# One exponential for both directions of a chunked scan: a predicated copy in PSUM in place of additive bars

## The chip, the cores and the metric

The kernel runs on one core of one Trainium2 chip. The time is the device time of one execution in microseconds (us). One execution of the kernel before was recorded by the hardware profiler; the rows below come from it. Engines are named as the profile names them: PE is TensorE's matmul side and PEld its weight loads, DVE is VectorE, ACT is ScalarE, POOL is GpSimd, SP issues most of the transfers. A number such as L1104 is a line of the kernel before.

## What is computed

The program is one layer of an encoder block: a modulated RMS norm, one input projection, grouped-query attention, a bidirectional Mamba-2 scan, two output projections merged by gates, and an MLP. The change touches the scan alone. Its part of the reference, cut:

```python
def segsum(a):
    cs = jnp.cumsum(a, axis=-1)
    diff = cs[..., :, None] - cs[..., None, :]
    return jnp.where(tril_mask, diff, -jnp.inf)

def ssd_chunked(xdt, a, bm, cm):                   # chunks of 128 positions
    CB = jnp.einsum("bclgn,bcsgn->bgcls", Cc, Bc)
    M = CB[:, :, None] * jnp.exp(segsum(A))
    y_diag = jnp.einsum("bgrcls,bcsgrp->bclgrp", M, X)
    ...                                            # states, carried from chunk to chunk
    return y_diag + y_off

y = ssd_chunked(forward) + flip(ssd_chunked(flipped, backward)) + ssd_D[:, None] * xf
```

Within a chunk, an output position l takes from a position s at or before it with the forward weights and from a position s at or after it with the backward weights. A pair off the diagonal therefore has one of the two weights, and a pair on the diagonal has both: there the difference of the cumulated sums is zero, so each direction's weight is that direction's dt times CB.

## The kernel before

The sequence of 1024 positions is 8 chunks of 128; the 32 scan heads are 4 groups of 8. The stage in question runs two streams that are woven into one order for PE: `scan()`, which goes through 4 x 8 = 32 pairs of group and chunk, and `products()`, which does the last gate columns and the two output projections, 24 matmuls of 128x512 for each half tile (L206 to L208). PE's order is fixed by `weave`, which takes the next piece from the stream that is behind by the planned costs. The orders of the other engines are set by the scheduler of the framework from dependences and priorities. Every engine runs its own list in order.

For one pair, `scan_load` loads the chunk, multiplies B and C to CB (PSUM tile `psm`, L1089) and lets ACT copy it to `cb` (L1091). `scan_w` is called twice, for four heads each. For each direction d it puts a block of 128x512 into a PSUM tile `psd`: first a product of the identity `identr` with `bars[d]` (L1104), which writes 0 where the direction counts and -1e30 where it doesn't; then a product of `st` and `mv` (L1105), which adds the differences of the cumulated sums (and the logarithm of dt). ACT takes the exponential into an SBUF tile `e` (L1107). DVE adds the two `e` tiles to `w` and multiplies `w` by `cb` (both recorded on the helper's line L154). There are two `psd` buffers, so a direction's product waits for the exponential of the same direction in the call before.

The rest of a pair follows one turn of the loop later. `scan_off` starts the output `u` on POOL as x times D (`Dbc`) and adds the two carried parts: a product `pso` on PE (L1122), a scaling `yo` on DVE, an addition on POOL. `scan_state` carries the forward state (`prevf`), `bwd_stream` prepares the backward states of the next group (`prevb`). `scan_y` multiplies `w` by x (`psy`, L1148), DVE adds it to `u`, POOL multiplies by `sz`, and one turn later PE transposes `u` (`psm`, L1158) in `scan_out`. The tiles `psm`, `pso`, `pst` and `psy` share four PSUM buffers (`psx`). While the second output projection begins, `load_g` fetches the finished scan results and splits them: `gh` on ACT (L1014), `gl` on DVE (L1015).

Of the kernel before, what the change touches and what calls it, by code (L numbers as in the profile page):

```python
# [9 lines left out]
F32 = mybir.dt.float32  # L10
F32R = mybir.dt.float32r
BF16 = mybir.dt.bfloat16
AF = mybir.ActivationFunctionType
ALU = mybir.AluOpType
# [4 lines left out]
P = 128  # L19
S = 1024  # L20
D = 1024
# [4 lines left out]
HD = 64  # L26
# [30 lines left out]
M2 = {mybir.EngineType.PE}  # L57
LEAD3 = 400
BIG = 1.5 * 2.0 ** 15
BAR = 1e30  # L60


def weave(tc, *streams, lead=0):
# [27 lines left out]
def block(ctx: ExitStack, tc: tile.TileContext, ia, out, upto=99, dbg=None):  # L91
    nc = tc.nc
    V, A, G, T = nc.vector, nc.scalar, nc.gpsimd, nc.tensor
# [39 lines left out]
    ident, GT, LT, LE, GE = (masks[:, i, :] for i in range(5))  # L133
# [12 lines left out]
    dt = sp.tile([P, NT, 64], F32, name="dt")  # L146
# [3 lines left out]
    def bc(ap, shape):  # L150
        return ap.to_broadcast(shape)

    def tt(e, o, a, b, op):
        e.tensor_tensor(out=o, in0=a, in1=b, op=op)  # L154
# [102 lines left out]
    with tc.tile_pool(name="p0", bufs=1) as p0, tc.tile_pool(name="ps0", bufs=1, space=PSUM) as ps0:  # L257
# [4 lines left out]
        ps = ps0.tile([P, 512], F32, name="psv", tag="psv", bufs=2)  # L262
# [97 lines left out]
        ps = ps0.tile([P, 512], F32, name="psv", tag="psv", bufs=2)  # L360
# [56 lines left out]
    with tc.tile_pool(name="p1", bufs=1, reuse_waits="tile") as p1, \  # L417
# [16 lines left out]
        identr = p1.tile([P, P], F32R, name="identr")  # L434
# [582 lines left out]
    with tc.tile_pool(name="p4", bufs=1, reuse_waits="tile") as p4, \  # L1017
# [8 lines left out]
        for q in range(2):  # L1026
            dma(pick[20 + 4 * q:24 + 4 * q], ia["pick"][0:4])

        identr = p4.tile([P, P], F32R, name="identr")
        V.tensor_copy(identr, ident)  # L1030
        bars = [p4.tile([P, 4, P], F32R, name=f"bar{d}") for d in range(2)]
        for d, m in enumerate((LE, GE)):
            V.tensor_scalar(out=bars[d], in0=bc(m.unsqueeze(1), [P, 4, P]), scalar1=-1.0, scalar2=BAR, op0=ALU.add, op1=ALU.mult)
        for i in range(2):
            for d in range(2):

# [3 lines left out]
        Dbc = p4.tile([P, NSH], F32, name="Dbc")  # L1040
# [25 lines left out]
        def scan_load(g, c):  # L1066

            hs = slice(8 * g, 8 * g + 8)
            e = dict(g=g, c=c, hs=hs)
            xb = p4.tile([P, 640], F32, name="xb", tag="xb", bufs=2)  # L1070
            dma(xb, xb_d[g][:, c])
            e["xt"], bt = xb[:, 0:512].rearrange("p (h d) -> p h d", h=8), xb[:, 512:640]
            bcT = p4.tile([P, 2, P], F32, name="bcT", tag="bcT", bufs=2)
            dma(bcT, bc_d[g][:, :, c * P:(c + 1) * P])
            bT, e["cT"] = bcT[:, 0], bcT[:, 1]
            e["st"], e["mv"] = cst[cnt[0] % 2], cmv[cnt[0] % 2]
            cnt[0] += 1
            r0 = c * 8 + 2 * g
            for d in range(2):
                dma(e["st"][d][0:28].bitcast(F32), cn_d[d][:, r0:r0 + 2])  # L1080
                dma(e["mv"][d][4:20:5].bitcast(F32), cr_d[d].rearrange("q (h r) l -> q h r l", h=4)[:, :, r0:r0 + 2])
            e["prevb"] = None
            if c < 7:
                e["prevb"] = p4.tile([P, 8, HD], F32, name="pbl", tag="pbl", bufs=2)
                dma(e["prevb"].rearrange("p h d -> p (h d)"), pb_d[g][c])
            e["sz"] = p4.tile([P, 512], F32, name="sz", tag="sz", bufs=2)
            dma(e["sz"], z_d[g][:, c])
            ps = ps4.tile([P, 512], F32, name="psm", tag="psx", bufs=PSX)
            T.matmul(ps[:, :P], bT, e["cT"], start=True, stop=True)  # L1089
            e["cb"] = p4.tile([P, P], F32, name="cb", tag="cb", bufs=2)  # L1090
            A.copy(e["cb"], ps[:, :P])  # L1091
            if c < 7:
                e["xd"] = p4.tile([P, 8, HD], F32, name="xdf", tag="xd", bufs=3)
                tt(G, e["xd"], e["xt"], bc(dec["sf"][:, c, hs].unsqueeze(2), [P, 8, HD]), ALU.mult)
            e["bt"] = bt
            e["w"] = []
            return e

        def scan_w(e, hh):

            ex = []
            for d in range(2):
                pd = ps4.tile([P, 512], F32, name="psd", tag="psd", bufs=2)
                T.matmul(pd, identr, bars[d].rearrange("p h l -> p (h l)"), start=True, stop=False)  # L1104
                T.matmul(pd.rearrange("p (h l) -> p h l", h=4), e["st"][d][:, hh], e["mv"][d][:, :, hh], start=False, stop=True)  # L1105
                ex.append(p4.tile([P, 4, P], F32, name="e", tag="e", bufs=3))
                A.activation(ex[d].rearrange("p h l -> p (h l)"), pd, AF.Exp)  # L1107
            wh = p4.tile([P, 4, P], F32, name="w", tag="w", bufs=4)
            e["w"].append(wh)
            tt(V, wh, ex[0], ex[1], ALU.add)  # L1110
            tt(V, wh, wh, bc(e["cb"].unsqueeze(1), [P, 4, P]), ALU.mult)

        def scan_off(e, prev, ed):

            c, hs = e["c"], e["hs"]
            if "u" not in e:
                e["u"] = p4.tile([P, 8, HD], F32, name="u", tag="u", bufs=2)
                tt(G, e["u"], e["xt"], bc(Dbc[:, hs].unsqueeze(2), [P, 8, HD]), ALU.mult)
            if prev is None:
                return  # L1120
            po = ps4.tile([P, 8, HD], F32, name="pso", tag="psx", bufs=PSX)
            T.matmul(po.rearrange("p h d -> p (h d)"), e["cT"], prev.rearrange("p h d -> p (h d)"), start=True, stop=True)  # L1122
            t = p4.tile([P, 8, HD], F32, name="yo", tag="yo", bufs=2)
            tt(V, t, po, bc(ed[:, c, hs].unsqueeze(2), [P, 8, HD]), ALU.mult)
            tt(G, e["u"], e["u"], t, ALU.add)
# [51 lines left out]
        def scan():  # L1177
# [5 lines left out]
            for g in range(NG):  # L1183
                bw = bwd_stream(g + 1) if g + 1 < NG else iter(())
                for c in range(NT + (2 if g == NG - 1 else 0)):
                    e = None
                    if c < NT:
                        e = scan_load(g, c)
                        yield 0.43
                        scan_w(e, 0)  # L1190
                        yield 0.43
                    if p:
                        scan_off(p, f, dec["ef"])
                        yield 0.85
                    if o:
                        scan_out(o)
                        pipe["done"] += 1
                        yield 0.85
                    if p:
                        scan_off(p, p["prevb"], dec["eb"])  # L1200
                        yield 0.85
                        f = scan_state(p, f)
                        yield 0.85
                    if e:
                        scan_w(e, 1)
                        yield 0.43
                    if p:
                        scan_y(p)
                        yield YC
                    if next(bw, None):  # L1210
                        yield 0.85
                    o, p = p, e
# [40 lines left out]
    with tc.tile_pool(name="p5", bufs=1, reuse_waits="tile") as p5, \  # L1253
# [41 lines left out]
        for n, (i, second) in enumerate(jobs):  # L1295
# [12 lines left out]
            for half in range(2):  # L1308
                ps = part[i][half] if i in part else ps5.tile([P, 512], F32, name="psg", tag="psg", bufs=6)
# [39 lines left out]
    with tc.tile_pool(name="p6", bufs=1, reuse_waits="tile") as p6:  # L1349
# [9 lines left out]
        def turned(hf, k):  # L1359
            ps = ps7.tile([P, 512], F32, name="pst", tag="ps1", bufs=4)  # L1360
            for j in range(4):
                T.transpose(ps[:, j * P:(j + 1) * P], x1[hf * 4 + j][:, k * P:(k + 1) * P], ident)
            return ps
# [4 lines left out]
        for t in range(NT):  # L1368
# [3 lines left out]
            for n in range(2):  # L1372
# [3 lines left out]
                ps = ps7.tile([P, 512], F32, name="pso", tag="ps2", bufs=4)  # L1376
# [12 lines left out]
            if t == 4:  # L1389
                for k in range(KT):  # L1390
                    ps = turned(0, k)
# [404 lines left out]
```

## Time and profile before

| | us |
|---|---|
| median of 3 runs | 2523.82 |
| the 3 runs | 2523.82, 2516.72, 2524.56 |
| the profiled execution | 2523.71 |
| its span, first to last instruction | 2521.9 |
| PE busy in the span | 2418.8 (96%) |
| DVE busy | 1724.4 (68%) |
| ACT busy | 1125.7 (45%) |
| POOL busy | 867.8 (34%) |

The profiled execution lies at the median, and 1.8 us of it lie outside the span. PE is busy nearly everywhere; the scan stage is the stretch from about 1229 to 1641 us. A matmul's busy time includes the part in which the next one already runs, so what a matmul takes of PE's time is read from the distance between starts.

### The profile page before, as it was taken

How to read it: one execution, taken by the hardware profiler on the slowest of the kernel's cores; microseconds unless marked ns; L12 is line 12 of the kernel's file. 1: busy time of each engine (PE TensorE's matmuls, PEld its weight loads, DVE VectorE, ACT ScalarE, POOL GpSimd, SP SyncE). 2: the span in 40 equal slices, each digit the busy share in tenths (PEclk: the TensorE clock that was granted, in tenths of full speed). 3: DMA queues.
4: the chain of work that ended last, by engine and by line, in shares of the span. 5: the costliest groups of instructions: out<-in, count | busy, mean ns of one | idle time of the engine just before them, and what ended most of it. 6: DMA issues, size and time to landing. Idle time of an engine off the chain costs nothing. (4 is left out here: it accounts for less than half of the span.)

```text
span 2521.9 us, 32355 instructions
## 1 busy us (share of the span) xinstructions
PE 2418.8 (96%) x11403; PEld 1937.3 (77%) x11403; DVE 1724.4 (68%) x2199; ACT 1125.7 (45%) x1944; POOL 867.8 (34%) x672
## 2 busy tenths in 40 slices
PE   5899999999999999999899999998998999999999
PEld 5898777888867777777577767776776888888887
DVE  5756345777766666666577787546569888667794
ACT  5455522555466666666333444343233222264430
POOL 3210107666501111110356565514017866113200
PEclk9899999999999999999999999999999999999999
DMA  7654661333622222111766665466414544564422
GB/s 261 187 163 130 211 202 61 99 101 117 193 96 80 63 75 69 51 57 38 250 198 204 187 207 170 130 225 196 145 65 163 201 153 164 191 198 141 152 84 88
DMA packets 282162, 363.38 MB, mean 144 GB/s; under 512 B 33673, under 2 KB 166513, under 8 KB 282001
## 3 DMA queue, kind: packets, MB, share of 16 engines
q1 hardware_dynamic: 209841, 285.22, 36.2%
q10 hardware_dynamic: 72160, 76.11, 9.1%
q8 instruction: 90, 1.47, 0.3%
q14 instruction: 71, 0.58, 0.1%
HBM read 248.18 MB, written 113.06 MB: 143 GB/s over the span
## 5 line engine op out<-in xcount | busy, mean ns | idle before, releaser
L892 DVE TENSOR_REDUCE nm<-pss 128x1 f32<-128x1024 f32 x128 | 156.6, 1224 | 133.9 <-PE pss L890 132.4
L380 PE MATMUL psq<-twl,hh 128*128 128x400 f32 (+1 forms) x512 | 194.2, 381 | 5.5 <-DVE twl L154 4.8
L379 PE MATMUL psq<-twh,hh 128*128 128x400 f32 (+1 forms) x512 | 193.5, 383 | 3.4 <-ACT qkvr L512 1.2
L381 PE MATMUL psq<-twh,hl 128*128 128x400 f32 (+1 forms) x512 | 192.7, 378 | 0.2 <-DVE hl L154 0.2
L894 ACT ACTIVATE pf<-pss,nm 128x1024 f32<-128x1024 f32 x128 | 142.8, 1115 | 102.0 <-PE pst L905 99.3
L154 DVE TENSOR_TENSOR pl<-pst,ph 128x512 fp32r<-128x512 f32 x256 | 167.8, 683 | 27.6 <-ACT ph L168 27.6
L905 PEld LDWEIGHTS pst<-masks,pf 128*128 128x128 f32 x1024 | 118.4, 140 | 70.0 <-issue 29.6
L168 ACT CAST ph<-pst 128x512 fp32r<-128x512 f32 x256 | 146.4, 585 | 54.2 <-PE pst L905 41.0
L905 PE MATMUL pst<-masks,pf 128*128 128x128 f32 x1024 | 157.0, 276 | 11.7 <-DVE pl L154 9.7
L1673 PE MATMUL p<-o,o 128*128 128x512 f32 x400 | 153.6, 390 | 2.2 <-DVE ac L154 1.4
L1674 PE MATMUL p<-o,o 128*128 128x512 f32 x400 | 155.3, 389 | 0.2 <-DVE o L154 0.2
L154 POOL TENSOR_TENSOR av<-av,rz 64x512 f32<-64x512 f32 x32 | 41.5, 1298 | 326.6 <-DMA rz<-rz 168.3
L1675 PE MATMUL p<-o,o 128*128 128x512 f32 x400 | 153.7, 389 | 0.0
L714 DVE SCALAR_TENSOR_TENSOR tap<-pad,cwT,tap 128x1024 f32<-128x1024 f32 x96 | 123.4, 1285 | 5.1 <-ACT tap L712 3.7
L168 ACT CAST wop<-ws 128x512 fp32r<-128x512 f32 x116 | 71.8, 620 | 112.7 <-PE pp L1333 77.3
L380 PEld LDWEIGHTS psq<-twl,hh 128*128 128x128 f32 x512 | 99.0, 193 | 18.1 <-DVE twl L154 5.8
L154 POOL TENSOR_TENSOR sl<-sl 128x512 f32<-128x512 f32 x32 | 49.6, 1553 | 178.5 <-DVE o L154 72.2
L379 PEld LDWEIGHTS psq<-twh,hh 128*128 128x128 f32 x512 | 98.5, 193 | 16.0 <-ACT qkvr L512 1.7
L381 PEld LDWEIGHTS psq<-twh,hl 128*128 128x128 f32 x512 | 98.3, 192 | 12.7 <-issue 0.9
L168 ACT CAST o<-sl 128x512 fp32r<-128x512 f32 x92 | 56.9, 623 | 105.4 <-PE p L1675 88.2
L1107 ACT ACTIVATE e<-psd 128x512 f32<-128x512 f32 x128 | 70.8, 595 | 73.2 <-PE psd L1105 66.8
L942 PE MATMUL pv<-pl,v 128*64 128x512 f32 x256 | 102.0, 419 | 0.0
(424 smaller groups left out, 7068.3 us busy)
## 6 DMA issues: line engine op xcount, KB each, us to landing
ar<-r SPq DMA_DIRECT2D x100, 256.0 KB
wada<-in_w_ada_dram SPq DMA_DIRECT2D x48, 512.0 KB
r<-in_w_mlp_dram SPq DMA_DIRECT2D x32, 512.0 KB
sl<-in_w_mlp_dram SPq DMA_DIRECT2D x64, 256.0 KB
r<-in_w_in_dram SPq DMA_DIRECT2D x26, 512.0 KB
r<-ro ACTq DMA_DIRECT2D x52, 256.0 KB
r<-as SPq DMA_DIRECT2D x48, 256.0 KB
xb<-cst ACTq DMA_DIRECT2D x20, 512.0 KB
```

The costliest lines, as they stand in the source:

```text
L154: e.tensor_tensor(out=o, in0=a, in1=b, op=op)
L168: (e_hi or A.copy)(hi, src)
L379: T.matmul(o, hhi[k][half][:, sl], hi[:, k % 2, :n], start=k == 0, stop=False)
L380: T.matmul(o, hhi[k][half][:, sl], lo[:, k % 2, :n], start=False, stop=False)
L381: T.matmul(o, hlo[k][half][:, sl], hi[:, k % 2, :n], start=False, stop=k == KT - 1)
L714: V.scalar_tensor_tensor(out=tap, in0=pad[:, k:k + S], scalar=cwT[:, 24 * k + i:24 * k + i + 1], in1=tap, op0=ALU.mult, op1=ALU.add)
L892: V.tensor_reduce(out=nm, in_=ps, axis=AX.X, op=ALU.max, negate=True)
L894: A.activation(pfs[u], ps, AF.Exp, bias=nm, accum_out=zall[:, u:u + 1])
L905: T.transpose(pt[:, k], pf[:, (hf * 4 + k) * P:(hf * 4 + k + 1) * P], ident)
L1673: T.matmul(ps, a[:, 0, sl], b[0], start=start, stop=False)
L1674: T.matmul(ps, a[:, 0, sl], b[1], start=False, stop=False)
L1675: T.matmul(ps, a[:, 1, sl], b[0], start=False, stop=stop)
```

## The change

`scan_w` no longer writes bars. Both directions' differences go to PSUM as they are, one matmul each. Then one predicated copy on DVE writes the second direction's difference over the first's in the PSUM tile, where a mask `below` (t > s, made once as int32) is set. ACT takes one exponential of the joined tile straight into `w`, and DVE multiplies by `cb` as before. The identity in the matmul's type and the two bar tiles are gone.

On the diagonal the joined tile holds the forward difference only. The backward direction's share there, dt times CB's diagonal, is added to D: in `scan_load` one DVE instruction multiplies CB by the identity and sums each row (`cd`), and a second makes `Dd` = dt x `cd` + D for the eight heads. `scan_off` then starts `u` from `Dd` in place of `Dbc`.

```diff
-        identr = p4.tile([P, P], F32R, name="identr")
-        V.tensor_copy(identr, ident)
-        bars = [p4.tile([P, 4, P], F32R, name=f"bar{d}") for d in range(2)]
-        for d, m in enumerate((LE, GE)):
-            V.tensor_scalar(out=bars[d], in0=bc(m.unsqueeze(1), [P, 4, P]), scalar1=-1.0, scalar2=BAR, op0=ALU.add, op1=ALU.mult)
+        below = p4.tile([P, P], mybir.dt.int32, name="below")
+        V.tensor_copy(below, GT)
...
             A.copy(e["cb"], ps[:, :P])
+
+            dg = p4.tile([P, P], F32, name="dg", tag="dg", bufs=2)
+            cd = p4.tile([P, 1], F32, name="cd", tag="cd", bufs=2)
+            V.scalar_tensor_tensor(out=dg, in0=ps[:, :P], scalar=1.0, in1=ident, op0=ALU.mult, op1=ALU.mult, accum_out=cd)
+            e["D"] = p4.tile([P, 8], F32, name="Dd", tag="Dd", bufs=3)
+            V.scalar_tensor_tensor(out=e["D"], in0=dt[:, c, 32 + 8 * g:40 + 8 * g], scalar=cd, in1=Dbc[:, hs], op0=ALU.mult, op1=ALU.add)
...
-            ex = []
+            pd = [ps4.tile([P, 4, P], F32, name="psd", tag="psd", bufs=2) for d in range(2)]
             for d in range(2):
-                pd = ps4.tile([P, 512], F32, name="psd", tag="psd", bufs=2)
-                T.matmul(pd, identr, bars[d].rearrange("p h l -> p (h l)"), start=True, stop=False)
-                T.matmul(pd.rearrange("p (h l) -> p h l", h=4), e["st"][d][:, hh], e["mv"][d][:, :, hh], start=False, stop=True)
-                ex.append(p4.tile([P, 4, P], F32, name="e", tag="e", bufs=3))
-                A.activation(ex[d].rearrange("p h l -> p (h l)"), pd, AF.Exp)
+                T.matmul(pd[d], e["st"][d][:, hh], e["mv"][d][:, :, hh], start=True, stop=True)
+            V.copy_predicated(pd[0], bc(below.unsqueeze(1), [P, 4, P]), pd[1])
             wh = p4.tile([P, 4, P], F32, name="w", tag="w", bufs=4)
             e["w"].append(wh)
-            tt(V, wh, ex[0], ex[1], ALU.add)
+            A.activation(wh, pd[0], AF.Exp)
             tt(V, wh, wh, bc(e["cb"].unsqueeze(1), [P, 4, P]), ALU.mult)
...
-                tt(G, e["u"], e["xt"], bc(Dbc[:, hs].unsqueeze(2), [P, 8, HD]), ALU.mult)
+                tt(G, e["u"], e["xt"], bc(e["D"].unsqueeze(2), [P, 8, HD]), ALU.mult)
```

On PE, around the first call of `scan_w` of a chunk, the order before reads as follows (`psg` are the woven products, `bar` the bars).

```order
L1089 MATMUL psm<-bcT 128x128
L206 MATMUL psg<-ah_0_10877,whi 128x512
L207 MATMUL psg<-al_0_10893,whi 128x512
L208 MATMUL psg<-ah_0_10877,wlo 128x512
L1104 MATMUL psd<-bar_10859,identr 128x512
L1105 MATMUL psd<-cmv_10849,cst_10845 128x512
L1104 MATMUL psd<-bar_10860,identr 128x512
L1105 MATMUL psd<-cmv_10850,cst_10846 128x512
L1122 MATMUL pso<-prevf,bcT 128x512
```

The same place in the order of the changed kernel (lines are one to five lower there, and the tiles' numbers are shifted by the tiles that are gone):

```order
L1085 MATMUL psm<-bcT 128x128
L205 MATMUL psg<-ah_0_10873,whi 128x512
L206 MATMUL psg<-al_0_10889,whi 128x512
L207 MATMUL psg<-ah_0_10873,wlo 128x512
L1105 MATMUL psd<-cmv_10849,cst_10845 128x512
L1105 MATMUL psd<-cmv_10850,cst_10846 128x512
L1121 MATMUL pso<-prevf,bcT 128x512
```

Two matmuls of every call are gone, 128 of 9192 rows in all, and nothing else on PE changes its place.

On DVE, one whole turn of the loop before, with what each instruction waits for in brackets (`prevb` belongs to the next group's backward states, `w<-e` is the addition of the two exponentials):

```order
L154 TENSOR_TENSOR prevb<-prevb,pst 128x512 [waits PE_49]
L154 TENSOR_TENSOR prevb<-prevb,cb 128x512 [waits DMAHW4_49,DVE_49]
L154 TENSOR_TENSOR w<-e 128x512 [waits Activation_49]
L154 TENSOR_TENSOR yo<-pso,ef 128x512 [waits PE_49]
L154 TENSOR_TENSOR w<-w,cb 128x512 [waits DVE_49]
L154 TENSOR_TENSOR yo<-pso,eb 128x512 [waits PE_49]
```

And the same place after the change (`dg,cd` is the diagonal's sum, `Dd` the new D):

```order
L153 TENSOR_TENSOR prevb<-prevb,pst 128x512 [waits PE_49]
L153 TENSOR_TENSOR prevb<-prevb,cb 128x512 [waits DMAHW4_49,DVE_49]
L1091 SCALAR_TENSOR_TENSOR dg,cd<-psm,masks 128x128 [waits Activation_49]
L1106 COPY_PREDICATED psd<-below,psd 128x512 [waits PE_49]
L1093 SCALAR_TENSOR_TENSOR Dd<-dt,cd,Dbc 128x8 [waits DVE_49]
L153 TENSOR_TENSOR yo<-pso,ef 128x512 [waits PE_49]
L153 TENSOR_TENSOR w<-w,cb 128x512 [waits Activation_49]
L153 TENSOR_TENSOR yo<-pso,eb 128x512 [waits PE_49]
```

The addition, which waited for ACT, has given its place to a copy that waits for PE; the multiplication, which waited for DVE itself, now waits for ACT; and the diagonal's sum stands ahead of the copy and waits for ACT's copy of CB.

## Rows read from the trace of the kernel before

**Rows 1.** Busy time per engine in stretches of the scan stage (us).

```profile
core 0: us, PE busy (x) PEld busy (x) DVE busy (x) ACT busy (x) POOL busy (x), PEclk, DMA share, GB/s
1229.00:1250.00 21.00, 15.62 (x44) 8.91 (x43) 16.41 (x22) 7.07 (x12) 7.79 (x7) 0.84 1.03 354
...
1300.00:1350.00 50.00, 50.00 (x240) 37.39 (x239) 34.61 (x44) 17.95 (x38) 32.23 (x25) 1.00 0.64 198
...
1450.00:1500.00 50.00, 45.25 (x198) 31.46 (x197) 44.08 (x53) 23.60 (x46) 30.27 (x21) 0.97 0.70 220
```

**Rows 2.** PE in order of time around a call: start us, duration us, engine, line.

```profile
1350.88 0.39 PE L1104 MATMUL psd<-bar,identr 128*128 128x512 f32 x1
1351.11 0.39 PE L1105 MATMUL psd<-cmv,cst 128*128 128x512 f32 x1
1351.33 0.39 PE L1104 MATMUL psd<-bar,identr 128*128 128x512 f32 x1
1351.56 0.40 PE L1105 MATMUL psd<-cmv,cst 128*128 128x512 f32 x1
...
1357.42 0.39 PE L1105 MATMUL psd<-cmv,cst 128*128 128x512 f32 x1
...
1361.87 0.40 PE L1104 MATMUL psd<-bar,identr 128*128 128x512 f32 x1
```

**Rows 3.** Groups of the stage: busy us, mean ns | idle before, its releasers.

```profile
L1107 ACT ACTIVATE e<-psd 128x512 f32<-128x512 f32 x128 | 70.8, 595 | 73.2 <-PE psd L1105 66.8 <-DMA y<-gts 5.9
L154 DVE TENSOR_TENSOR w<-e 128x512 f32<-128x512 f32 x64 | 62.1, 970 | 46.1 <-ACT e L1107 45.7
L1104 PE MATMUL psd<-bar,identr 128*128 128x512 f32 x128 | 55.4, 433 | 4.1 <-ACT e L1107 4.1
L154 DVE TENSOR_TENSOR w<-w,cb 128x512 f32<-128x512 f32 x64 | 56.6, 885 | 1.4
```

**Rows 4.** Who waited for whom, 1250 to 1641 us: us in total, times, longest.

```profile
DVE w L154 <- ACT e L1107: 45.7, 39, 2.5
```

**Rows 5.** Busy time as in rows 1, over the scan turns as a whole.

```profile
1250.00:1641.00 391.00, 380.67 (x1810) 285.50 (x1809) 284.52 (x344) 155.87 (x317) 222.57 (x165) 0.99 0.60 183
```

**Rows 6.** DVE instructions by tile: durations in ns, least/median/longest.

```profile
L154 DVE TENSOR_TENSOR w<-e x64: 678/694/1767, 1259.1 to 1624.5; 128x512 f32<-128x512 f32 x64
L154 DVE TENSOR_TENSOR u<-u,psy x32: 673/681/689, 1271.1 to 1632.5; 128x512 f32<-128x512 f32 x32
```

**Rows 7.** Groups elsewhere in the program that stand near the new instructions.

```profile
L530 DVE RECIPROCAL dz<-dz 128x512 f32<-128x512 f32 x1 | 3.4, 3352 | 0.0
L1268 DVE TENSOR_SCALAR dg<-masks,rs 128x128 f32<-128x128 f32 x8 | 1.9, 280 | 0.0
L160 DVE TENSOR_SCALAR rs_v<-st 128x8 f32<-128x8 f32 x1 | 0.2, 173 | 0.0
L1153 ACT ACTIVATION_READ_ACCUMULATOR sqj<-u 128x1 f32 x32 | 6.2, 193 | 0.0
```

**Rows 8.** In order of time, the tightest of the usual turns: from `psy` to the transposes.

```profile
1591.24 1.89 PE L1148 MATMUL psy<-xb,w 128*128 128x64 f32 x16
...
1594.63 1.29 POOL L154 TENSOR_TENSOR u<-u,sz 128x512 f32<-128x512 f32 x1 [3.92 <-DVE u L154]
...
1597.11 0.49 PE L1158 MATMUL psm<-masks,u 128*128 128x128 f32 x3
```

**Rows 9.** In order of time, the first two calls of the stage.

```profile
1254.19 0.40 PE L1105 MATMUL psd<-cmv,cst 128*128 128x512 f32 x1
...
1258.00 1.09 ACT L1107 ACTIVATE e<-psd 128x512 f32<-128x512 f32 x2
1258.65 0.28 PEld L1104 LDWEIGHTS psd<-bar,identr 128*128 128x128 f32 x1 [4.50 <-ACT e L1107]
```

**Rows 10.** In order of time, the turn in which `load_g` shares DVE.

```profile
1471.18 0.40 PE L1105 MATMUL psd<-cmv,cst 128*128 128x512 f32 x1
...
1480.70 0.68 DVE L154 TENSOR_TENSOR w<-e 128x512 f32<-128x512 f32 x1
...
1483.76 1.12 PE L1158 MATMUL psm<-masks,u 128*128 128x128 f32 x4 [3.03 <-POOL u L154]
```

More of the change, by code (lines that the diff above doesn't have):

```diff
@@ L59 @@
 BIG = 1.5 * 2.0 ** 15
-BAR = 1e30
 def weave(tc, *streams, lead=0):
```

## The prediction

> **What bounds the kernel now.** I looked first at the busy time of the engines by stretches of the scan stage. In an ordinary stretch PE is busy all of its 50 us at the full granted clock (1.00, the 2.4 GHz level), while DVE has 34.61 us of work, ACT 17.95 and POOL 32.23 [rows 1]. Two stretches are otherwise: the 21 us of the stage's start, where PE is busy for 15.62 and the transfers fill their share (1.03), and 1450 to 1500, where DVE has 44.08 us of work and PE 45.25 [rows 1]. So PE sets the pace nearly everywhere, DVE in one short place, transfers at the start.
>
> Then I looked at PE in order of time, to see what a matmul costs when PE is full. The four matmuls of a call start at 1350.88, 1351.11, 1351.33 and 1351.56 although each lasts 0.39 to 0.40 [rows 2]. They overlap; from start to start one takes (1351.56 - 1350.88) / 3 = 0.227 us. That is the price of a matmul here.
>
> Last I followed the one loop that could take over: PE writes `psy`, DVE adds it to `u`, POOL multiplies, PE transposes. In the tightest of the usual turns `psy` starts at 1591.24, POOL is done at 1594.63 + 1.29 = 1595.92, and PE comes to the transposes at 1597.11 [rows 8]: 1.2 us are left, and PE doesn't wait.
>
> **PE: 128 matmuls fewer.** Each of 64 calls loses two matmuls with the bars (128 in the trace [rows 3]); PE's order is otherwise the same. Where PE is full this is 128 x 0.227 = 29.1 us. The busy column gives 55.4 us for the same 128 [rows 3], nearly twice as much, since it counts the overlap.
> The Trainium skill (Trainium Kernel Development and Optimization, Performance Expectations) says that matmul busy time is a bad measure since matmuls are pipelined; the starts bear it out (0.227 between starts against 0.39 of duration [rows 2]), and by the busy column the sum would be 26 us lower.
>
> **ACT: 64 exponentials fewer**, 64 x 0.595 = 38 us of work [rows 3]. ACT isn't full (155.87 of 391 us [rows 5]), so this is worth nothing by itself.
>
> **DVE: an addition becomes a predicated copy, and two small instructions come in.** The 64 additions go: 62.1 us [rows 3]. No row shows a predicated copy. Nearest is an instruction on the same 128x512 that reads one operand from PSUM, the addition of `psy`: 0.681 [rows 6]. The costliest instruction of the trace on this shape is a reciprocal with 3.352 [rows 7]. I take 0.68, since the copy, like the addition of `psy`, reads one operand from each memory and computes nothing, and keep 3.35 as the other end. It can't be much below 0.67, the least that any such instruction shows [rows 6], so no gain hides there. 64 x 0.68 = 43.5 us.
>
> One thing of the rows speaks for 0.68 rather than the 0.970 that the addition takes on average. The addition reads both operands from SBUF and lasts from 0.678 to 1.767; the addition of `psy`, with one from PSUM, never lasts more than 0.689, while POOL works as much beside it [rows 6].
> The Trainium skill (SBUF — State Buffer, Who interferes with whom) has a rule for it: a DVE instruction with two SBUF inputs contends with a GpSimd instruction that reads SBUF, one with at most one SBUF input doesn't. The trace agrees (1.767 against 0.689 at the longest [rows 6]); without the rule, at 0.970, the copies would be 62.1 us and DVE's sum 18.6 higher, which still leaves it below PE's.
>
> The diagonal's sum per chunk: a 128x128 instruction, 0.28, with a read of its accumulator, for which ACT's 0.193 stands; the new D, 128x8, 0.173 [rows 7]. Together 0.65, for 32 chunks 20.7 us; 10 and 40 us are the bounds, the lower without any separate read and with the two halves cheaper, the upper if each took double.
>
> DVE's sum over the turns of the scan: 284.5 [rows 5] - 62.1 + 43.5 + 20.7 = 286.6 us, about what it was, in 391 - 29 = 362 us: 79% in place of 73%. So DVE stays below PE, with 75 us to spare.
>
> **The new waits.** Before, PE got a `psd` buffer back from ACT alone. Now both come back only when DVE has copied and ACT has taken the exponential, so what is queued ahead of the copy on DVE can hold PE. From the last matmul of one call to the first of the next are 1361.87 - 1357.42 = 4.45 us [rows 2], all of other work that stays. The new chain needs 0.40 for the matmul, 0.68 for the copy, 0.60 for the exponential, and 0.1 for each of three handovers (PE goes on at 1258.65, 0.1 after the first of the two exponentials that take 1.09 from 1258.00 [rows 9]): 2.0 us. So some 2.5 us of DVE's queue can stand ahead of the copy before PE feels it. At 39 of the 64 additions DVE had nothing else to do and waited for ACT [rows 4], so there the copy will find DVE free; at the other 25 it stands behind one or two instructions of 0.7 to 1.1 us. I cost this at nothing outside the two places below.
>
> The diagonal's sum waits for ACT's copy of CB, and the copy stands behind it on DVE; ACT's copy may itself stand behind the square of `u`, which waits for POOL. That shifts the copy by under 1 us in a usual turn, inside the 2.5. The multiplication by `cb` now waits for ACT, some 0.9 us after the copy; those idle pieces of DVE, 64 at most, replace the 45.7 us in which it waited for the exponentials [rows 4].
>
> POOL does the same work; its first instruction for `u` waits for the new D, which is ready long before, since it is used one turn later. PSUM's shared buffers are held by `psm` until the diagonal's sum is done, four allocations ahead of the next use. The loop of rows 8 loses the two bar matmuls of one call, 0.45 of its 1.2 us, and still holds. SP's loads are the same in number, and a chunk's bytes come in 7% less time at a share of 0.64 [rows 1]: room enough.
>
> **What is not gained.** At the start PE stands from 1254.19 to 1258.65 until ACT, which waits for transfers, has taken the first exponential [rows 9]. The two bars ahead of that wait (0.45 us) are lost in it, and the copy with its handover (1.0) comes into the chain: 1.5 us. Around 1446 to 1484, where `gl` crowds DVE, PE waits for the chain through DVE already now: the call whose last matmul started at 1471.18 had its addition at 1480.70, 9.5 us later, and PE waited 3.03 for `u` at 1483.76 [rows 10]. There DVE sets the pace, so the bars of three turns, 12 x 0.227 = 2.7 us, are lost, and PE can't run 9.5 us ahead any more, since the copy holds `psd`: I add the same wait once more, 3.0. Together 7.2.
>
> **Sum.** 2523.7 of the profiled execution - 29.1 + 7.2 = 2501.8. That execution lies 0.1 us under the median of the runs, so the forecast for the median is **2502 us**, 0.9% faster. A time within 0.3% (7.6 us) of before couldn't be told from no change.
>
> **Rivals.**
> 1. *Full gain and more.* The copies are steady at 0.68 where the additions took up to 1.77 [rows 6]; if that alone frees DVE in the crowded stretch, its 3.03 wait and the half-speed restart behind it (some 2 us) go as well: 2523.7 - 29.1 - 5 = 2490. Against it: the diagonal's instructions put back what the copies save.
> 2. *PE waits for `psd`.* If each of the 25 calls at which DVE was late [rows 4] holds PE for 0.4 us more, 10 us are given back: 2512. It decides as soon as more than 2.5 us stand ahead of the copy on DVE.
> 3. *Slower: the predicated copy is a slow instruction.* DVE's other work is 284.5 - 62.1 + 20.7 = 243 us, so with 391 us to fill [rows 5] two copies a turn cost as much as was gained at (391 - 243) / 64 = 2.3 us each, or 1.6 if DVE keeps the 45.7 us of waiting that it has now [rows 4]. At the reciprocal's 3.35 DVE needs 243 + 214 = 457 us: 2523.7 + 66 = 2590. For it: the instruction isn't in the trace, and it reads and writes PSUM. Against it: every streaming instruction of this shape on DVE lies near 0.7.
> 4. *No change:* the bars cost nothing because PE waits anyway. Rows 1 speak against it; only the two stretches above have such waits. It would come about with a copy of 1.6 to 2.3 us: 2516 to 2531.
>
> **How the numbers follow.** The forecast (2495 to 2508) gets 0.62, rival 1 (2489 to 2495) 0.14, rival 2 (2508 to 2516) 0.12, no change 0.07, slower 0.05. Faster by over 0.3% is the first three: 0.88. The range is 2490 to 2516: its lower end is rival 1, its upper end rival 2, and 0.12 and a little of rival 1 lie outside.
>
> **What would show it.** Right: PE's starts in a usual turn keep their distances with two gaps of 0.227 less in each call; a copy at about 0.68 with hardly any spread; DVE near 287 us over the scan; from 1229 to the end of the stage about 390 in place of 412 us. Wrong: a copy above 1.6 us; matmuls of L1105 that wait for ACT's exponential in usual turns; transposes that wait for POOL in many turns and not in three.

## The result and the profile after

The changed kernel takes 2496.7 us (median of four runs, 2495.3 to 2499.4) against 2522.3 for the kernel before on the same chip: a ratio of 0.9903, 95% interval 0.989 to 0.9916. That is 25.6 us less; 21.9 were forecast. The profiled execution took 2497.45 us, its span 2495.7. The lines of the kernel after stand one to five lower than those of before.

First the busy time by stretches, the columns as in [rows 1]; the second row is the scan's turns, to be held against [rows 5].

```profile
1229.00:1250.00 21.00, 15.15 (x38) 8.64 (x37) 14.28 (x20) 7.40 (x12) 6.23 (x5) 0.76 1.00 337
1250.00:1616.00 366.00, 356.59 (x1703) 264.79 (x1703) 282.42 (x444) 126.64 (x255) 226.81 (x167) 1.00 0.65 196
1300.00:1350.00 50.00, 50.00 (x247) 37.84 (x246) 38.62 (x59) 15.55 (x32) 32.70 (x26) 1.00 0.69 208
1450.00:1500.00 50.00, 46.53 (x216) 32.85 (x215) 44.70 (x68) 18.14 (x37) 35.77 (x25) 1.00 0.65 203
```

PE is still full in an ordinary stretch, and DVE now has 38.62 of 50 us where it had 34.61. Over the turns DVE's sum is what it was (282.42 against 284.52), in 366 us in place of 391.

PE in order of time around two calls (start us, duration us, engine, line): the two matmuls of a call take 1350.02 - 1349.56 = 0.46 us from start to start of the next work, in place of four with 0.227 each [rows 2].

```profile
1344.14 0.62 PE L1105 MATMUL psd<-cmv,cst 128*128 128x512 f32 x2
1344.60 1.90 PE L1147 MATMUL psy<-xb,w 128*128 128x64 f32 x16
...
1349.56 0.62 PE L1105 MATMUL psd<-cmv,cst 128*128 128x512 f32 x2
1350.02 0.40 PE L205 MATMUL psg<-ah,whi 128*128 128x512 f32 x1
```

DVE's groups that changed (busy us, mean ns | idle before, its releaser), 1250 to 1616 us:

```profile
L153 DVE TENSOR_TENSOR w<-w,cb 128x512 f32<-128x512 f32 x64 | 57.9, 905 | 8.4 <-ACT w L1109 7.6
L1106 DVE COPY_PREDICATED psd<-below,psd 128x512 f32<-128x512 int32 x64 | 44.0, 688 | 4.0 <-PE psd L1105 4.0
L1093 DVE SCALAR_TENSOR_TENSOR Dd<-dt,cd,Dbc 128x8 f32<-128x8 f32 x32 | 13.5, 422 | 0.4
L1091 DVE SCALAR_TENSOR_TENSOR dg<-psm,masks 128x128 f32<-128x128 f32 x32 | 9.1, 285 | 8.4 <-ACT cb L1087 8.4
L1091 DVE DVE_READ_ACCUMULATOR dg<-psm,masks 128x1 f32 x32 | 2.6, 82 | 0.0
```

The spread of two of them (ns: least/median/longest, as in [rows 6]):

```profile
L1106 DVE COPY_PREDICATED psd<-below,psd x64: 681/687/697, 1257.3 to 1595.8; 128x512 f32<-128x512 int32 x64
L1093 DVE SCALAR_TENSOR_TENSOR Dd<-dt,cd,Dbc x32: 208/225/1243, 1257.9 to 1589.2; 128x8 f32<-128x8 f32 x32
```

Who waited for whom in the same stretch (us in total, times, longest). The fourth row is the new wait that rival 2 stood on.

```profile
ACT w L1109 <- DVE psd L1106: 113.5, 47, 5.9
...
DVE dg L1091 <- ACT cb L1087: 8.4, 13, 1.5
DVE w L153 <- ACT w L1109: 7.6, 12, 1.2
...
PE psd L1105 <- DVE psd L1106: 4.3, 3, 2.8
```

ACT waits a great deal for the copies; that costs nothing, since ACT isn't the bound. PE waited for a copy three times, 4.3 us in all, 2.8 of it at the start of the stage.

**Where the time went.** The start of `psy` marks a turn. The first, the 15th, the 19th and the 31st of before:

```profile
1269.13 1.90 PE L1148 MATMUL psy<-xb,w 128*128 128x64 f32 x16
...
1436.88 1.89 PE L1148 MATMUL psy<-xb,w 128*128 128x64 f32 x16
...
1489.73 1.89 PE L1148 MATMUL psy<-xb,w 128*128 128x64 f32 x16
...
1623.66 1.89 PE L1148 MATMUL psy<-xb,w 128*128 128x64 f32 x16
```

The same four of after:

```profile
1268.27 1.89 PE L1147 MATMUL psy<-xb,w 128*128 128x64 f32 x16
...
1423.39 1.89 PE L1147 MATMUL psy<-xb,w 128*128 128x64 f32 x16
...
1471.70 1.89 PE L1147 MATMUL psy<-xb,w 128*128 128x64 f32 x16
...
1594.64 1.89 PE L1147 MATMUL psy<-xb,w 128*128 128x64 f32 x16
```

The first fourteen turns took 167.75 us and now take 155.12: 12.6 us less, and 14 x 4 x 0.227 is 12.7. The last twelve took 133.93 and now take 122.94: 11.0 less, and 12 x 4 x 0.227 is 10.9. These turns shrank by the price of four starts each, and by nothing else. The four between, where `load_g` crowds DVE, took 52.85 and now take 48.31: 4.5 less, where 3.6 would be the full price.

The last matmul of the stage with `gh`, of before and, below, of after:

```profile
1662.77 0.39 PE L1313 MATMUL psg<-gh,wlo 128*128 128x512 f32 x1
```

```profile
1633.93 0.39 PE L1312 MATMUL psg<-gh,wlo 128*128 128x512 f32 x1
```

There the kernel after is 28.84 us ahead, of 29.1 that the matmuls are worth; 0.86 of it is an earlier first `psy`, which differs from execution to execution (the profile of e7, below, is 31.2 ahead at this place, its first `psy` 3.8 us earlier than before's). The spans differ by 26.2 only: 2.6 us were lost later, in work that the change doesn't touch. e7 shows that this belongs to the execution.

### The profile page after: what moved, and what is told of

It reads as the page before. It is cut to its first block, busy times and chain, and to the rows that moved or that the text cites. A ratio compares the mean times of both kernels' runs of the same rounds, so it can differ in the third digit from the quotient of the medians.

```text
span 2495.7 us, 32129 instructions
## 1 busy us (share of the span) xinstructions
PE 2393.4 (96%) x11275; PEld 1916.6 (77%) x11275; DVE 1717.7 (69%) x2293; ACT 1096.2 (44%) x1880; POOL 872.2 (35%) x672
## 5 line engine op out<-in xcount | busy, mean ns | idle before, releaser
L153 DVE TENSOR_TENSOR pl<-pst,ph 128x512 fp32r<-128x512 f32 x256 | 167.9, 683 | 27.8 <-ACT ph L167 27.8
L153 DVE TENSOR_TENSOR o<-sl,o 128x512 fp32r<-128x512 f32 x92 | 72.4, 790 | 40.3 <-ACT o L167 40.3
```

## The experiments

Edits are against the kernel after, except e2. The table puts the distances between `psy` starts of all of them side by side (us; each from one profiled execution), and the medians of the runs.

| kernel | turns 0 to 14 | 14 to 18 (crowded) | 18 to 30 | median us | ratio to before, 95% |
|---|---|---|---|---|---|
| before | 167.8 | 52.8 | 133.9 | 2522.3 | |
| after | 155.1 | 48.3 | 122.9 | 2496.7 | 0.9903 (0.989 to 0.9916) |
| e7, after again | 155.1 | 48.8 | 123.0 | 2493.7 | 0.9891 (0.9876 to 0.9906) |
| e1, bars back | 167.9 | 50.0 | 133.8 | 2522.7 | 1.0007 (0.9996 to 1.0017) |
| e2, before without bars | 155.0 | 50.0 | 123.0 | 2494.9 | 0.9899 (0.9883 to 0.9914) |
| e3, half the bars | 161.5 | 53.2 | 128.3 | 2512.8 | 0.9964 (0.9954 to 0.9974) |
| e4, no diagonal | 155.0 | 46.9 | 123.0 | 2496.3 | 0.9903 (0.9887 to 0.992) |
| e5, copy twice | 157.6 | 54.0 | 123.9 | 2506.8 | 0.9939 (0.9925 to 0.9954) |
| e6, copy three times | 166.2 | 69.2 | 130.6 | 2537.7 | 1.0054 (1.0037 to 1.0071) |

### e1: the bars put back, all else as after

```diff
+                T.matmul(pd[d].rearrange("p h l -> p (h l)"), identr, bars[d].rearrange("p h l -> p (h l)"), start=True, stop=False)
-                T.matmul(pd[d], e["st"][d][:, hh], e["mv"][d][:, :, hh], start=True, stop=True)
+                T.matmul(pd[d], e["st"][d][:, hh], e["mv"][d][:, :, hh], start=False, stop=True)
```

> The changed kernel with the 128 matmuls of the bars put back ahead of the differences; the predicated copy, the one exponential and the diagonal's part stay, and the result is the same (the copy overwrites where the bar stands). If the gain is PE's time (128 starts of 0.227 us), it goes: 2497 + 29 = 2526, between 2518 and 2530. If it came from ACT's 64 exponentials or from steadier work on DVE, the time stays within 4 us of 2497.

The median of ten runs is 2522.7 us, against 2521.1 for before on this chip: no difference. With its copies, its single exponential and its diagonal in place, but with the 128 matmuls, the kernel is as slow as before. So the matmuls brought the gain: the 64 exponentials and the steadier copies are worth nothing by themselves that these runs could tell. Its first and its 15th `psy` are as far apart as before's to 0.1 us (167.86 against 167.75):

```profile
1266.12 1.90 PE L1154 MATMUL psy<-xb,w 128*128 128x64 f32 x16
...
1433.98 1.90 PE L1154 MATMUL psy<-xb,w 128*128 128x64 f32 x16
```

### e2: before, without the bars, with its two exponentials and its addition

```diff
-                T.matmul(pd, identr, bars[d].rearrange("p h l -> p (h l)"), start=True, stop=False)
-                T.matmul(pd.rearrange("p (h l) -> p h l", h=4), e["st"][d][:, hh], e["mv"][d][:, :, hh], start=False, stop=True)
+                T.matmul(pd.rearrange("p (h l) -> p h l", h=4), e["st"][d][:, hh], e["mv"][d][:, :, hh], start=True, stop=True)
-                A.activation(ex[d].rearrange("p h l -> p (h l)"), pd, AF.Exp)
+                A.activation(ex[d].rearrange("p h l -> p (h l)"), pd, AF.Exp, scale=0.0)
```

> The kernel before with the bars' 128 matmuls left out and nothing else moved: two exponentials, the addition of the two on DVE, D as before. The exponential gets a scale of 0, so that unmasked differences stay finite; mask and decay are left out of the result. If the gain is PE's time alone: 2494 to 2500, as the changed kernel. If the copy in place of the contended addition (0.687 against 0.970 us) or ACT's relief is needed for it: 2508 to 2522.

The median is 2494.9 us, 26.3 under before of the same chip. Taking the matmuls out of before (its result then lacks mask and decay) gains all that the change gains, and the change pays nothing for its copies, handovers and diagonal that could be told here (2494.9 against 2496.7 and 2493.7 for the kernel after). Its first and its 15th `psy` lie 155.00 apart:

```profile
1265.72 1.89 PE L1147 MATMUL psy<-xb,w 128*128 128x64 f32 x16
...
1420.72 1.89 PE L1147 MATMUL psy<-xb,w 128*128 128x64 f32 x16
```

### e3: the bars for one direction alone

```diff
+                if d == 0:
+                    T.matmul(pd[d].rearrange("p h l -> p (h l)"), identr, bars[d].rearrange("p h l -> p (h l)"), start=True, stop=False)
-                T.matmul(pd[d], e["st"][d][:, hh], e["mv"][d][:, :, hh], start=True, stop=True)
+                T.matmul(pd[d], e["st"][d][:, hh], e["mv"][d][:, :, hh], start=d == 1, stop=True)
```

> The changed kernel with the bars of the forward direction alone put back, 64 matmuls. PE's time: half of 29, so 2511, between 2507 and 2516. If the removed matmuls were partly hidden (as the 7.2 us of the prediction were), the first 64 cost clearly more or less than the second 64 of the run with all bars.

In the usual turns the price is linear to the tenth: 161.47 us for the first fourteen (rows below), midway between 155.1 and 167.8. The whole is not linear: e3 gained 8.3 us against before of its chip where half of 26 would be 13. Putting back the first 64 matmuls thus cost 16 to 19 us (against 2496.7 and 2493.7), the second 64 cost 9.9 (to e1), and half the gain would be a ratio of about 0.995, outside the interval. Why is not shown. The difference doesn't lie in the usual turns: the profiled execution, the slowest of the nine, has its first `psy` late (1274.47) and the slowest crowded turns of these kernels but for e5 and e6 (53.2). With nine runs from 2506.3 to 2517.0 and one profile, neither can be put down to the edit.

```profile
1274.47 1.90 PE L1155 MATMUL psy<-xb,w 128*128 128x64 f32 x16
...
1435.94 1.89 PE L1155 MATMUL psy<-xb,w 128*128 128x64 f32 x16
```

### e4: the diagonal's second part left out

```diff
-            dg = p4.tile([P, P], F32, name="dg", tag="dg", bufs=2)
-            cd = p4.tile([P, 1], F32, name="cd", tag="cd", bufs=2)
-            V.scalar_tensor_tensor(out=dg, in0=ps[:, :P], scalar=1.0, in1=ident, op0=ALU.mult, op1=ALU.mult, accum_out=cd)
-            e["D"] = p4.tile([P, 8], F32, name="Dd", tag="Dd", bufs=3)
-            V.scalar_tensor_tensor(out=e["D"], in0=dt[:, c, 32 + 8 * g:40 + 8 * g], scalar=cd, in1=Dbc[:, hs], op0=ALU.mult, op1=ALU.add)
...
-                tt(G, e["u"], e["xt"], bc(e["D"].unsqueeze(2), [P, 8, HD]), ALU.mult)
+                tt(G, e["u"], e["xt"], bc(Dbc[:, hs].unsqueeze(2), [P, 8, HD]), ALU.mult)
```

> The changed kernel without the diagonal's two DVE instructions; u starts from D alone, so the backward direction's share on the diagonal is left out of the result. If they are hidden on DVE as costed: 2494 to 2498. If they hold the copy behind ACT's copy of CB and so PE: up to 32 x 0.65 = 21 us less, 2476 to 2490.

The median is 2496.3 us, beside 2496.7 and 2493.7 with the diagonal: it costs nothing that could be told here. The row 1300 to 1420 (columns as in [rows 1]) of after, and below it that of e4, shows 7.4 us less work on DVE and PE full in both.

```profile
1300.00:1420.00 120.00, 120.00 (x579) 89.54 (x578) 93.35 (x148) 36.81 (x78) 78.36 (x60) 1.00 0.68 207
```

```profile
1300.00:1420.00 120.00, 120.00 (x577) 89.26 (x576) 85.99 (x116) 37.35 (x79) 79.82 (x60) 1.00 0.69 209
```

### e5 and e6: the copy two and three times

The second and third copy write the same values again: this doubles and triples the one new DVE instruction of a call.

```diff
             V.copy_predicated(pd[0], bc(below.unsqueeze(1), [P, 4, P]), pd[1])
+            V.copy_predicated(pd[0], bc(below.unsqueeze(1), [P, 4, P]), pd[1])
```

> The changed kernel with every predicated copy made twice, the same data both times. DVE's work over the scan rises from 282 to 326 us of 366, and psd is held 0.69 us longer. If DVE's time has room and 2.5 us can stand ahead of the copy: 3 to 10 us more, 2500 to 2507. If PE waits on the copy at every call: 64 x 0.69 = 44 us more, 2541.

> Three predicated copies in place of one, so 2.06 us a call, inside the 1.6 to 2.3 us at which the prediction put the turning point. DVE's work is 282 + 88 = 370 us, as long as the scan now takes. If the turning point was right: 2515 to 2535, near the time before. If PE waits on each copy: 2585. If DVE's idle pieces hide nearly all: below 2508.

The second copy brings 64 x 0.688 = 44.0 us of work to DVE, and the kernel takes 2506.8: 13.1 us more than the kernel after beside it (e7). The third brings as much again, and 2537.7: 30.9 more, slower than before and a little above the 2535 at which the expectation ended. About half of the dearer second step lies in the crowded turns (15.2 us more from e5 to e6, against 5.1 from e7 to e5). Rows 1430 to 1510 (columns as in [rows 1]) of before:

```profile
1430.00:1510.00 80.00, 75.25 (x347) 54.39 (x346) 66.27 (x78) 37.34 (x73) 47.56 (x34) 0.98 0.69 212
```

of after:

```profile
1430.00:1510.00 80.00, 76.06 (x355) 54.39 (x354) 73.80 (x107) 31.24 (x61) 57.10 (x40) 1.00 0.71 219
```

of e5, with PE's waits for `psd` there (as in [rows 4]):

```profile
1430.00:1510.00 80.00, 73.20 (x326) 52.80 (x327) 72.65 (x112) 31.80 (x61) 50.42 (x36) 0.96 0.66 207
...
PE psd L1105 <- DVE psd L1107: 4.0, 3, 1.8
PE psd L1105 <- ACT w L1110: 1.6, 3, 0.8
```

of e6, with its waits and four of its matmuls:

```profile
1430.00:1510.00 80.00, 65.88 (x258) 48.18 (x257) 63.34 (x99) 27.39 (x52) 32.92 (x26) 0.81 0.59 180
...
PE psd L1105 <- DVE psd L1108: 7.4, 3, 4.5
PE psd L1105 <- ACT w L1111: 6.6, 4, 3.7
...
1449.96 0.80 PE L1105 MATMUL psd<-cmv,cst 128*128 128x512 f32 x1 [4.46 <-DVE psd L1108]
1452.71 0.80 PE L1105 MATMUL psd<-cmv,cst 128*128 128x512 f32 x1 [1.96 <-ACT w L1111]
1453.31 0.63 PE L205 MATMUL psg<-ah,whi 128*128 128x512 f32 x1
1453.73 0.63 PE L206 MATMUL psg<-al,whi 128*128 128x512 f32 x1
```

In e6 PE stands for 80 - 65.88 = 14.1 us of this stretch (3.9 in the kernel after), and the granted clock is 0.81 in place of 1.00: after the waits of 4.46 and 1.96 a `psd` matmul lasts 0.80, twice the usual 0.39 to 0.40, and the next starts are 0.42 us apart in place of 0.227, so PE is at the lower of its two levels there. In this trace the granted clock is 0.50 for 30.7 of the 80 us, in three pieces; PE is busy for 25.1 of these, so the clock costs it some 12.5 us more, nearly as much as the waits themselves. A wait of PE is thus paid nearly twice in these turns. The other half of the second step lies in the 26 usual turns (8.6 and 6.8 us in the table): there PE now waits for copies and exponentials ahead of `psd` too, 6.5 us in all where e5 has 0.4, and the clock of the first fourteen turns is 0.98. These waits and the clock don't add up to all of the 15.4; the rest is not explained here.

### e7: the kernel after, once more, beside e5 and e6

> The changed kernel itself, for a second profile. The first one had gained 28.8 us by the end of the scan and 26.2 at the end. If the 2.6 us are lost by the change (later stages start at another place of their loads), this profile shows them again between 1634 and 1900 us; if they vary from execution to execution, it shows another figure. Time 2495 to 2500.

The median is 2493.7 us, 28.2 under before on this chip. In its profiled execution the turns are as in the first profile to within 0.6 us, and the stretch from the end of the stage to the program's last matmul takes 854.7 us, against 854.4 in before and 857.0 in the first profile of after. Over all nine profiled executions this stretch lies between 853.8 and 857.7, in no order of the changes made, and the kernel after has 2.4 us of difference with itself. That is where the 2.6 us went.

## Why the prediction was right, and where it was off

**The price and the mechanism: right.** PE set the pace, and a matmul was worth its distance of starts: 12.6 and 11.0 us measured in 26 usual turns, against 12.7 and 10.9 worked out. e1 and e2 show it for the whole kernel from two sides, e3 in the usual turns. From 1229 us to the end of the scan it took 28.8 us less than the 412 of before, where 390 in all had been forecast: some 383. PE's busy time over the whole program fell from 2418.8 to 2393.4 us, so by 25.4, near the gain; the durations of the removed group add up to 55.4 [rows 3].

**ACT: right.** Its group fell from 70.8 to 38.2 us, and e1, which keeps that, gains nothing.

**DVE: right in its sum, off in its parts.** Its sum over the turns is 282.42 us where 286.6 was forecast. The copy takes 0.687 where 0.68 was taken, and never more than 0.697, with POOL busy for 226.81 of 366 us beside it. The Trainium skill (SBUF — State Buffer, Who interferes with whom) let one expect that of an instruction with a single SBUF input, and the trace agrees again (0.697 at the longest, against 1.767 for the addition it replaced [rows 6]). The diagonal costs 0.285 + 0.082 + 0.422 = 0.79 us a chunk, 25.2 in all, not 20.7: the accumulator's read is cheaper than ACT's (0.083 against 0.193), but the 128x8 instruction isn't 0.173. It has two inputs from SBUF, and where POOL is at work it can last until POOL is done (below). The 25.2 are inside the bounds of 10 and 40, and e4 shows that they lie beside PE's work. The floor of 0.67 "that any such instruction shows" holds for the two groups of [rows 6] only: the trace of before has casts of 128x512 on DVE at 0.41. The copy isn't one of these, so nothing hung on it.

**The cushion ahead of a copy: right.** I took the start of each call's second matmul, of its copy and of the next call's first matmul from the trace of after, for all 64. The copy begins 0.95 us after the matmul in the median call, and the next call 5.1 us after it. Past the start and outside 1430 to 1510 the latest copy began 2.45 us after its matmul, and PE didn't wait. In the crowded stretch copies that began 4.80 and 6.64 us after it, at 1441.69 and 1462.49, held the next call for 0.20 and 1.34 us; two that began 4.66 and 5.08 us after it didn't hold its first matmul, since the next call came later too. The estimate was that 2.5 us could be stood, so it was on the safe side.

**The loop of [rows 8]: right.** In the usual turns no transposes waited for POOL. At the last two turns of the stage they did, for 0.28 and 1.44 us in the kernel after and 0.07 and 1.44 in before.

**What is not gained: the step that failed.** It put 7.2 us down as lost, 1.5 at the start and 5.7 in the crowded turns. By the medians 25.6, 28.2 (e7) and 26.3 (e2) were gained, so 0.9 to 3.5 of the 29.1 were not. The three terms:
- *The start, 1.5.* The chain went as described: PE waited for the copy, 2.8 us by the waits above. But the first `psy` lies anywhere from 1265.3 to 1274.5 in the nine profiled executions, and at 1268.3 and 1265.3 in the two of the kernel after. A term of 1.5 can't be told there, and stays open.
- *The bars of three turns, 2.7, and the 3.0 of a further wait.* The sum had made the four crowded turns 2.1 us longer. They are 4.5 us shorter than before's (4.0 in e7), and 1.7 shorter (1.2 in e7) than those of e1, which has all the bars; the full price is 3.6. So the 3.0 were lost by neither comparison. Whether the 2.7 were stays open: held against before nothing of the full price is missing, held against e1 some 2 us are, and each of these is one execution.

The step that failed is thus the adding up of two waits. PE's waits for DVE and POOL from 1430 to 1510 in before:

```profile
PE psm L1158 <- POOL u L154: 3.8, 3, 3.0
```

and in the kernel after, with the two longest of them in order of time:

```profile
PE psd L1105 <- DVE psd L1106: 1.5, 2, 1.3
PE psm L1157 <- POOL u L153: 1.3, 2, 1.0
...
1463.23 1.13 PE L1105 MATMUL psd<-cmv,cst 128*128 128x512 f32 x2 [1.34 <-DVE psd L1106]
...
1466.87 0.66 PE L1157 MATMUL psm<-masks,u 128*128 128x128 f32 x4 [0.96 <-POOL u L153]
```

The new wait for `psd` came, but the old one for POOL shrank: the single wait of 3.03 [rows 10] became 0.96. In all PE stands 3.9 us in the stretch (5.1 in e7), where it stood 4.75, and not 3.0 more. The prediction took the two waits as independent. Both come from the same late DVE queue; where PE already waits at `psd`, what it would wait for afterwards has come that much nearer. That explanation is argued; the sums of waits agree with it, but they don't prove it.

A few microseconds in this stretch can't be settled anyway: e1, e2, e3 and e4 have 50.0, 50.0, 53.2 and 46.9 there, and no order by DVE's work can be seen in them.

**The rivals.** The result lies between the forecast and rival 1, *full gain and more*, and the second median of the same kernel (e7, 2493.7) lies in the range given to rival 1: the gain was nearly full, but not more, and what rival 1 thought would bring it, the steadier copies, brings nothing that the medians show (e1). The granted clock of 1430 to 1510 did go from 0.98 to 1.00, worth at most 80 x 0.02 = 1.6 us, as rival 1 had it; in e2, without copies, it is 0.91 from 1450 to 1470, so this varies. Rival 2, PE waiting for `psd` in usual turns, didn't happen: 4.3 us in three places. Rival 3's turning point was placed well: e5, at 1.37 us for a call's copies, is 15.2 us faster than before, and e6, at 2.06, is 15.7 slower; on a line between them the gain is used up at 1.7 us, within the 1.6 to 2.3 forecast. Its mechanism is only half of what e6 shows: DVE isn't full there (348.38 of 395 us from 1250 to 1645), and what holds PE is single late copies and the clock that falls behind them. The slow copy itself failed to come.

**One reading that was too simple.** At the 39 additions for which DVE used to wait for ACT, it was to find the copy's turn free and then wait for ACT at the multiplication. Those waits are 7.6 us, 12 times, in place of 45.7: DVE reaches a copy when its matmuls are done already (it was idle ahead of one for 4.0 us, 6 times), and two instructions in front of the multiplication fill most of the time that the exponential takes. This cost and gained nothing.

## What to carry to other kernels

Price a matmul on a full PE by the distance between starts in a full stretch (here 0.227 us, not the 0.39 of its duration); the gain worked out by that price held to 1% in both stretches of usual turns. Work that moves from a full engine to one with room costs nothing while each buffer comes back in time: count the microseconds that its holder may be late, and look for the places where another stream already fills that engine. Where two waits come from the same late queue, take the larger of them and don't add them; that advice is argued here, not shown. Where the granted clock falls behind the waits, as in e6, they cost nearly twice what they last.

## What the hardware showed beside that

A predicated copy of 128x512 from PSUM to PSUM with a mask of 32-bit integers in SBUF takes 0.681 to 0.697 us, as much as an addition with one operand in PSUM [rows 6], and in e6 three in a row on the same block take the same each (0.677 to 0.697).

A DVE instruction of eight elements a partition can last 1.24 us. The row of DVE, and below it that of POOL at the same time, in the kernel after:

```profile
1456.39 1.24 DVE L1093 SCALAR_TENSOR_TENSOR Dd<-dt,cd,Dbc 128x8 f32<-128x8 f32 x1
```

```profile
1456.01 1.59 POOL L153 TENSOR_TENSOR u<-u,yo 128x512 f32<-128x512 f32 x1 [2.17 <-DVE yo L153]
```

POOL began 0.38 us earlier and was done at 1457.60; the DVE instruction ended at 1457.63. Of the 32, twelve lasted longer than 0.3 us, and each of them ended 0.02 to 0.03 us after an instruction that POOL had under way; the others took 0.21 to 0.23. So in these twelve cases the small size of the instruction, with both of its inputs in SBUF, was no protection from POOL.
